# RMSNorm and matmul on one core: tile 112 stored apart from tiles 113 to 115, in two pieces of 114 and 14 rows

## The chip, the cores and the metric

One core of one Trainium2 chip runs the kernel. The metric is device time in microseconds (us) of one execution, lower is better. Beside the timed runs there is one profiled execution, whose trace has every instruction of the five engines and every packet of the 16 DMA engines that serve the core.

## The reference

The input x has 16 x 1024 rows (tokens) of 512 float32 features. Each row is divided by its root mean square, multiplied by gamma, and taken through a 512 x 768 matrix:

```
rms = np.sqrt(np.mean(x ** 2, axis=-1, keepdims=True) + eps)
x_norm = x / rms * gamma
return np.matmul(x_norm, weight).astype(np.float32)
```

The output is 16,384 rows of 768 float32 numbers, 50.3 MB; x is 33.6 MB.

## The kernel before

The 16,384 rows are cut into 128 tiles of 128 rows (one row for each of the 128 partitions). A tile's product is 128 x 768, and each partition's piece of it is 3,072 bytes.

**Work on a tile.** x is loaded in groups of 4, 8 or 16 tiles (`load`). GpSimd casts x to bf16 (`cast`, L189), ScalarE takes the sum of squares (`square`, L197) and the root of the mean (`root`, L202), and VectorE its reciprocal. TensorE transposes the tile, two features at a time as one 32-bit word (`transpose_word`, L231), and VectorE copies the result out of PSUM (`evac`, L240). For four tiles in sixteen VectorE does the transpose itself in blocks of 32 x 32 (`move`, L272). Then TensorE multiplies by the weights (`product`, L301), which have gamma folded in, into one of three accumulators. `finish_tile` scales the product by the row's reciprocal root and writes it to a slot of the output buffer `ot`: even tiles on ScalarE (L280), odd tiles on VectorE (L282).

**Stores.** `ot` has four slots of eight tiles each (`OG` = 8, `OTS` = 4), used in turn. `finish_tile` calls `store` after each tile; `store` does nothing until the last tile of a stretch is there, and then issues one DMA on the SP queue (L294). The stretches come from `stretches` at L139: usually eight tiles, in the first group 1, 1, 2 and 4, in the group of tiles 112 to 119 4 and 4, in the last group 4, 2 and 2. The tile that ends a stretch also waits for the tile before it (`before` in `finish_tile`), so that the store has one engine to wait for.

**Rows in memory.** `rows` gives a block of tiles (32 of them from tile 32 on) interleaved rows: partition p of the block's tile t is row 32 p + t of the block. A store of n tiles is therefore 128 pieces of n x 3,072 bytes, each from one partition.

**Order.** The program is listed in the order of the code, and `Order.emit` sends it to the engines: it works out for each operation which earlier ones it needs, and puts waits on semaphores ahead of it on its own engine. The engines run their lists in order and meet only at those waits. A transfer gets a semaphore of its own while it is in flight. The loop over pairs of tiles (L406) sets what is queued behind what: casts, moves, norms and loads ahead, the transposes of a later pair fed between the matmuls of the pair at hand, then the two evictions with their stores. The SP queue carries the first loads (x up to tile 31, and the weights) and all 22 stores; the ScalarE queue carries gamma and the later loads. `emit` holds back the last store (tiles 126 and 127), which is issued after the other engines' ends are arranged; the waits for stores that nothing else waits for stand on ScalarE (`left`, L440).

Of the kernel before, what the change touches and what calls it, by code (L numbers as in the profile page):

```python
# [16 lines left out]
P = 128  # L17
# [83 lines left out]
def kernel(  # L101
# [9 lines left out]
    PE, DVE, ACT, POOL, SP = nc.tensor, nc.vector, nc.scalar, nc.gpsimd, nc.sync  # L111
    order = Order(tc)
# [5 lines left out]
    out = out.flatten_outer_dims()  # L118
# [5 lines left out]
    XG, OG = 16, 8  # L124
# [3 lines left out]
    def stretches(group, parts):  # L128
        first, size, i = {}, {}, 0
        for g in range(NT // group):  # L130
            for n in parts.get(g, [group]):
                for t in range(i, i + n):
                    first[t], size[t] = i, n
                i += n
        return first, size

    last = NT // OG - 1
    x_first, x_size = stretches(OG, {0: [4, 4]})
    o_first, o_size = stretches(OG, {0: [1, 1, 2, 4], last - 1: [4, 4], last: [4, 2, 2]})  # L139

    def rows(ap, i, n):
        base, t = (i - i % OG, OG) if OG <= i < XG else (x_first[i], x_size[i]) if i < OG else (i - i % XG, XG) if i < 2 * XG else (i - i % (2 * XG), 2 * XG)
        return ap[base * P:(base + t) * P, :].rearrange("(p t) d -> p t d", t=t)[:, i - base:i - base + n, :]

    def sb(name, shape, dtype):
        return nc.alloc_sbuf_tensor(name, shape, dtype).ap()
# [11 lines left out]
    ot = [sb(f"ot{n}", [P, OG, O], F32) for n in range(OTS)]  # L158
# [10 lines left out]
    def cells(name, slot, i, n=1):  # L169
        return [(name, slot, t) for t in range(i, i + n)]  # L170
# [115 lines left out]
    def accumulator():  # L286
        return next(turns) % 3

    def store(i):
        first, n = o_first[i], o_size[i]  # L290
        s = first // OG % OTS
        if i == first + n - 1:
            src = ot[s][:, first % OG:first % OG + n, :]
            order.transfer(SP, lambda: SP.dma_start(out=rows(out, first, n), in_=src), reads=cells("ot", s, first % OG, n))  # L294

    def hold(lhsT, of):
        run(PE, lambda: PE.ldweights(lhsT), of)  # L297
# [20 lines left out]
    def finish_tile(i, a, engine):  # L318
        s = i // OG % OTS

        before = [("ot", s, i % OG - 1)] if i == o_first[i] + o_size[i] - 1 else []
        scale(engine, ot[s][:, i % OG, :], ops[a][:, :O], rstd[:, i:i + 1],
              [("ops", a, 0), ("ops", a, 1), ("rstd", i)] + before, [("ot", s, i % OG)] + (opening if i == OG * (OTS - 1) else []))
        store(i)
# [158 lines left out]
```

## Time and profile before

| What | us |
|---|---|
| median of 3 runs | 209.56 |
| lowest and highest | 209.47, 212.21 |
| profiled execution, its own time | 209.04 |
| its span, first to last instruction | 206.97 |
| TensorE busy | 194.4 (94% of the span) |
| VectorE, ScalarE, GpSimd busy | 149.4, 144.5, 59.9 |
| mean granted TensorE clock | 0.980 of full speed |
| DMA: moved 85.62 MB, mean 414 GB/s | |

The stores' DMA issues, as the trace has them (start on SP), and when all of a store's semaphore counts had come in:

| Store of tiles | issued | landed |
|---|---|---|
| 104 to 111 | 176.86 | 191.49 |
| 112 to 115 | 183.06 | 195.11 |
| 116 to 119 | 189.24 | 198.74 |
| 120 to 123 | 193.93 | 202.38 |
| 124 and 125 | 196.53 | 204.22 |
| 126 and 127 | 199.40 | 206.06 |

How to read the profile: a row of 40 digits is the span in equal slices of 5.2 us, each digit the busy share in tenths. Only work counts as busy, not waits or the issuing of DMAs. The DMA share is the mean over the core's 16 DMA engines, so one engine that works while fifteen rest is 0.06. A DMA is cut into packets, each of which goes through one engine; a packet has a start, a duration and a size in the trace, but no engine's number. The page's line on DMA queues counts the packets of SP's queue (q1: 4176 packets, 60.29 MB), of ScalarE's (q10: 1732 packets, 25.17 MB), and of instruction fetches (q8: 7 packets, q14: 5). In the list of waits a line gives the waiting engine and line, what it waited for, the sum, the number of waits and the longest.

### The profile page before, as it was taken

How to read it: one execution, taken by the hardware profiler on the slowest of the kernel's cores; microseconds unless marked ns; L12 is line 12 of the kernel's file. 1: busy time of each engine (PE TensorE's matmuls, PEld its weight loads, DVE VectorE, ACT ScalarE, POOL GpSimd, SP SyncE). 2: the span in 40 equal slices, each digit the busy share in tenths (PEclk: the TensorE clock that was granted, in tenths of full speed). 3: DMA queues.
4: the chain of work that ended last, by engine and by line, in shares of the span. 5: the costliest groups of instructions: out<-in, count | busy, mean ns of one | idle time of the engine just before them, and what ended most of it. 6: DMA issues, size and time to landing. Idle time of an engine off the chain costs nothing.

```text
span 207.0 us, 2792 instructions
## 1 busy us (share of the span) xinstructions
PE 194.4 (94%) x1236; PEld 72.6 (35%) x717; DVE 149.4 (72%) x255; ACT 144.5 (70%) x343; POOL 59.9 (29%) x34
## 2 busy tenths in 40 slices
PE   6699999999999999999999999999999999999920
PEld 0134443442343334343344334433334333433300
DVE  0446556999579975999569975999569974999510
ACT  2698898777787687777777688677877687663310
POOL 1437751157005170062405151060701507000000
PEclk9799999999999999999999999999999999999995
DMA  5999999999999999999999999999999999999992
GB/s 206 423 439 437 399 404 422 427 441 427 424 437 424 440 420 423 431 431 439 413 440 423 424 445 412 443 418 420 443 418 434 431 437 426 423 442 404 416 423 121
DMA packets 5920, 85.62 MB, mean 414 GB/s; under 512 B 658, under 2 KB 660, under 8 KB 1556
## 3 DMA queue, kind: packets, MB, share of 16 engines
q1 hardware_dynamic: 4176, 60.29, 68.9%
q10 hardware_dynamic: 1732, 25.17, 28.5%
q8 instruction: 7, 0.11, 0.2%
q14 instruction: 5, 0.04, 0.0%
HBM read 35.13 MB, written 50.33 MB: 413 GB/s over the span
## 4 chain that ended last, share of the span: by engine, by line
PE 91%; DMA 2%; DVE 1%; ACT 1%; issue 0%; SPq 0%
PE ps L301 81%; PE ps L231 10%; DMA xt<-in_x_dram 2%; DVE ot L282 0%; ACT jk L197 0%; DVE xT L240 0%; DVE w_bf L282 0%; ACT ssq L202 0%; DVE rstd L204 0%; SPq L478 0%; SPq L437 0%
## 5 line engine op out<-in xcount | busy, mean ns | idle before, releaser
L301 PE MATMUL ps<-w_bf,xT 128*128 128x512 bf16 (+1 forms) x800 | 148.3, 327 | 0.5 <-DVE w_bf L282 0.5
L280 ACT ACTIVATE ot<-ps,rstd 128x768 f32<-128x768 f32 x64 | 57.6, 900 | 46.8 <-PE ps L301 46.7
L197 ACT ACTIVATE jk<-xt 128x512 bf16<-128x512 f32 x128 | 78.7, 618 | 3.1 <-DMA xt<-in_x_dram 3.1
L189 POOL CAST xb<-xt 128x2048 bf16<-128x2048 f32 (+3 forms) x21 | 46.4, 2218 | 114.5 <-PE ps L231 56.0
L282 DVE TENSOR_SCALAR ot<-ps,rstd 128x768 f32<-128x768 f32 x64 | 64.8, 1012 | 9.7 <-PE ps L301 9.2
L297 PEld LDWEIGHTS <-xT 128*128 128x128 bf16 x400 | 39.4, 98 | 59.9 <-issue 58.3
L231 PE MATMUL ps<-ident_f,xb 128*128 128x128 f32 x200 | 54.0, 273 | 1.7 <-POOL xb L189 1.6
L240 DVE COPY xT<-ps 128x1024 bf16<-128x1024 bf16 (+1 forms) x53 | 34.5, 653 | 26.2 <-PE ps L231 25.3
L272 DVE STREAM_TRANSPOSE xTq<-xq 32x256 f32<-32x256 f32 x112 | 48.8, 435 | 1.9
L231 PEld LDWEIGHTS ps<-ident_f,xb 128*128 128x128 f32 x200 | 28.1, 141 | 46.5 <-issue 43.6
L301 PE MATMUL ps<-w_bf,xTq 128*128 128x512 bf16 x224 | 42.8, 326 | 0.0
L197 ACT ACTIVATION_READ_ACCUMULATOR jk<-xt 128x1 f32 x128 | 24.3, 190 | 0.0
L297 PEld LDWEIGHTS <-xTq 128*128 128x128 bf16 x112 | 11.0, 98 | 14.5 <-issue 14.5
L261 POOL CAST xq<-xt 128x2048 bf16<-128x2048 f32 x7 | 13.3, 1893 | 0.0
L204 DVE RECIPROCAL rstd<-ssq 128x8 f32<-128x8 f32 (+3 forms) x20 | 3.8, 192 | 7.1 <-ACT ssq L202 6.9
L202 ACT ACTIVATE ssq<-ssq,eps_sb 128x8 f32<-128x8 f32 (+3 forms) x20 | 6.0, 300 | 0.6
L301 PE MATMUL ps<-ot 128*128 128x512 bf16 x10 | 4.3, 567 | 1.4 <-DVE eps_sb L355 1.4
L280 ACT ACTIVATE w_bf<-ot,g_sb 128x768 bf16<-128x768 f32 x2 | 1.9, 935 | 1.1 <-DMA ot<-in_weight_dram 1.1
L378 DVE COPY g_sb<-ps 128x4 f32<-128x4 f32 x1 | 0.2, 160 | 3.2 <-PE ps L372 3.2
L342 ACT ACT_TABLE_LOAD x1 | 1.3, 1283 | 1.5 <-SPq L437 1.5
L282 DVE TENSOR_SCALAR w_bf<-ot,g_sb 128x512 bf16<-128x512 f32 (+2 forms) x3 | 1.4, 481 | 0.6 <-DMA ot<-in_weight_dram 0.6
L372 PEld LDWEIGHTS ps<-ident_f,ot 2*128 2x128 f32 x2 | 0.3, 200 | 2.6 <-issue 2.6
(10 smaller groups left out, 1.9 us busy)
## 6 DMA issues: line engine op xcount, KB each, us to landing
out_dram<-ot SPq DMA_DIRECT2D x13, 3072.0 KB, 22.7
xt<-in_x_dram ACTq DMA_DIRECT2D x12, 2048.0 KB, 20.1
xt<-in_x_dram SPq DMA_DIRECT2D x3, 2048.0 KB, 17.7
out_dram<-ot SPq DMA_DIRECT2D x4, 1536.0 KB, 10.8
out_dram<-ot SPq DMA_DIRECT2D x3, 768.0 KB, 7.7
xt<-in_x_dram SPq DMA_DIRECT2D x2, 1024.0 KB, 6.9
ot<-in_weight_dram SPq DMA_DIRECT2D x2, 768.0 KB, 7.0
out_dram<-ot SPq DMA_DIRECT2D x2, 384.0 KB, 20.4
```

Source lines behind the costliest of these rows:

```text
L189: run(POOL, lambda: POOL.tensor_copy(out=xb[s][:, i % 8:i % 8 + n, :], in_=src), of, cells("xb", s, i % 8, n))
L197: run(ACT, lambda: ACT.activation(out=jk[n], in_=src[:, 0, :], func=AF.Square, accum_out=ssq[:, i:i + 1]), of, [("jk", n), ("ssq", i)])
L202: run(ACT, lambda: ACT.activation(out=ssq[:, s], in_=ssq[:, s], func=AF.Sqrt, scale=1.0 / D, bias=eps_sb), [("ssq", t) for t in range(i, i ...
L204: run(DVE, lambda: DVE.reciprocal(out=rstd[:, s], in_=ssq[:, s]), [("rms", i)], [("rstd", t) for t in range(i, i + n)])
L231: run(PE, lambda: PE.transpose(out=tp[b][:, t, h, :], in_=words[:, lo:lo + P], identity=ident_f), cells("xb", s, j % 4 * 2 + t) + ["ident" ...
L240: run(DVE, lambda: DVE.tensor_copy(out=dst[:, t:t + n, :], in_=src[:, t:t + n, :]), [("tp", b)], cells("xT", j % XTS, t, n))
L261: run(POOL, lambda: POOL.tensor_copy(out=xq[s], in_=src), of, [("xq", s)])
L272: run(DVE, lambda: DVE.transpose(out=dst, in_=src), [("xq", s)], [("xTq", s, n)])
L280: run(ACT, lambda: ACT.mul(out=dst, in_=src, mul=r), reads, writes)
L282: run(DVE, lambda: DVE.tensor_single_scalar(out=dst, in_=src, scalar=r, op=mybir.AluOpType.mult), reads, writes)
L297: run(PE, lambda: PE.ldweights(lhsT), of)
L301: run(PE, lambda: PE.add_instruction(mybir.InstMatmult(name=nc.get_next_instruction_name(), engine=mybir.EngineType.PE, ins=[PE.lower_ap(r ...
```

## The change

The group of tiles 112 to 119 is stored in stretches of 1, 3 and 4 tiles where it was 4 and 4. A stretch that begins at a tile named in `DIVIDED`, which is tile 112 alone, goes out as two DMAs, one of partitions 0 to 113 and one of partitions 114 to 127. All other stores are as before.

```
-    o_first, o_size = stretches(OG, {0: [1, 1, 2, 4], last - 1: [4, 4], last: [4, 2, 2]})
+    o_first, o_size = stretches(OG, {0: [1, 1, 2, 4], last - 1: [1, 3, 4], last: [4, 2, 2]})
...
+    DIVIDED = (112,)
+    PARTS = [slice(114), slice(114, P)]
+
     def store(i):
         first, n = o_first[i], o_size[i]
         s = first // OG % OTS
         if i == first + n - 1:
-            src = ot[s][:, first % OG:first % OG + n, :]
-            order.transfer(SP, lambda: SP.dma_start(out=rows(out, first, n), in_=src), reads=cells("ot", s, first % OG, n))
+            src, dst = ot[s][:, first % OG:first % OG + n, :], rows(out, first, n)
+            for part in PARTS if first in DIVIDED else [slice(0, P)]:
+                store_rows(dst[part], src[part], cells("ot", s, first % OG, n))
+
+    def store_rows(dst, src, of):
+        order.transfer(SP, lambda: SP.dma_start(out=dst, in_=src), reads=of)
```

## The prediction

> **What bounds the kernel now.** I read the page first, for the busy shares and for how the span is filled. These are its span and its rows of 40 slices.
>
> ```profile
> span 207.0 us, 2792 instructions
> ...
> PE   6699999999999999999999999999999999999920
> ...
> DMA  5999999999999999999999999999999999999992
> GB/s 206 423 439 437 399 404 422 427 441 427 424 437 424 440 420 423 431 431 439 413 440 423 424 445 412 443 418 420 443 418 434 431 437 426 423 442 404 416 423 121
> ```
>
> Two things are full from 10 us on: TensorE, and the 16 DMA engines together. TensorE stops two slices before the end and the DMA engines go on, so the end belongs to the stores. The waits of the SP queue say so too:
>
> ```profile
> SPq L294 <- DVE ot L282: 169.8, 19, 12.0
> ...
> SPq L478 <- DMA out_dram<-ot: 6.3, 1, 6.3
> ```
>
> SP mostly waits to be given a tile to store, and at the end it waits 6.3 us for the last store (tiles 126 and 127). The timeline of SP has that store's issue at 199.40, 0.3 us after VectorE finished tile 127. The busy table by stretch shows what those 6.3 us are (columns: length, PE, PEld, DVE, ACT, POOL, granted clock, DMA share, GB/s):
>
> ```profile
> 190.00:195.00 5.00, 5.00 (x33) 1.54 (x16) 3.05 (x5) 1.71 (x2) 0.00 (x0) 1.00 0.98 415
> 195.00:199.00 4.00, 3.05 (x20) 0.78 (x8) 1.93 (x2) 0.99 (x2) 0.00 (x0) 1.00 1.00 424
> 199.00:201.00 2.00, 0.00 (x0) 0.00 (x0) 0.10 (x1) 0.00 (x0) 0.00 (x0) 1.00 0.98 409
> 201.00:202.00 1.00, 0.00 (x0) 0.00 (x0) 0.00 (x0) 0.00 (x0) 0.00 (x0) 1.00 0.97 406
> 202.00:203.00 1.00, 0.00 (x0) 0.00 (x0) 0.00 (x0) 0.00 (x0) 0.00 (x0) 0.55 0.78 326
> 203.00:204.00 1.00, 0.00 (x0) 0.00 (x0) 0.00 (x0) 0.00 (x0) 0.00 (x0) 0.50 0.31 129
> 204.00:205.00 1.00, 0.00 (x0) 0.00 (x0) 0.00 (x0) 0.00 (x0) 0.00 (x0) 0.50 0.18 74
> 205.00:206.00 1.00, 0.00 (x0) 0.00 (x0) 0.00 (x0) 0.00 (x0) 0.00 (x0) 0.50 0.07 31
> ```
>
> The share falls in steps: all sixteen engines until 202, then 0.18 from 204 to 205, which is 0.18 x 16 = 3 engines. The packets that start from 203.7 on say the same:
>
> ```profile
> DMA packets 20, 0.10 MB, mean 52 GB/s; under 512 B 3, under 2 KB 3, under 8 KB 20
> ```
>
> A store ends on each engine with one packet of 4 bytes, for the semaphore. Three of them are left here, so three engines still have work. Thirteen are through by 203.65, the three end at 205.10, 205.48 and 205.72, and the program ends 1.25 us after the last. **The end is set by three late engines**, with idle time on thirteen others. The mean of the sixteen ends is 203.4, so no shift of rows can gain more than about 2.3 us.
>
> **The change, part by part.** Every load and store here of 128 rows is cut into 16 equal shares of 8 rows: 8 data packets and one semaphore packet on each engine. Gamma's load of two rows made two packets, on two engines at once. If 114 rows too are cut into equal shares over at most 16 engines, the most that divides 114 is 6, so six engines get 19 rows each; 14 rows go to 14 engines, one row each. Of tile 112, six engines then carry 20 rows, eight carry 1, and two none, where each had 8.
>
> Prices of a packet come from the trace: 121 ns for 3,072 bytes, 234 for 6,144, 460 for 12,288, and 9 for a semaphore. On one engine a packet starts 3 or 4 ns before the one ahead ends, so each takes 117.5, 230.5, 456.5 and 5.5 ns of the engine. No packet of 9,216 bytes is in the trace; 1.5 x 230.5 = 346 from the one side and 0.75 x 456.5 = 342 from the other bound it, and I take the middle, 344. One engine's work for tiles 112 to 115 is:
> - before: 8 x 456.5 + 5.5 = 3.66 us;
> - one of the six: 19 x 0.1175 + 0.1175 + 8 x 0.344 + 3 x 0.0055 = 5.12 us, so +1.46;
> - one with a single row: 0.1175 + 2.752 + 0.011 = 2.88 us, so -0.78;
> - one without: 2.76 us, so -0.90.
>
> Issues on SP go from one to three, 0.33 us each. On SP's timeline tile 112's two lie between the store of tiles 104 to 111 (issued at 176.86) and that of 113 to 115:
>
> ```profile
> 176.86 0.33 SPq L294 DMA_DIRECT2D out_dram<-ot  x1
> ...
> 183.06 0.33 SPq L294 DMA_DIRECT2D out_dram<-ot  x1
> ```
>
> and ScalarE's eviction of tile 112 stands in its own timeline:
>
> ```profile
> 177.06 0.90 ACT L280 ACTIVATE ot<-ps,rstd 128x768 f32<-128x768 f32 x1 [0.92 <-PE ps L301]
> ```
>
> ScalarE finishes tile 112 at 177.96; SP then waits for that, issues twice by 178.7, and is free 4.4 us before tile 115 is ready. Behind it on SP stand only the later stores, whose tiles come later still. The engines hold queued work then (the store of 104 to 111 lands up to 191.5), so the earlier issue brings nothing forward and delays nothing. Without that cover the two issues would cost 0.66 us. Tile 112's wait is now on ScalarE and no longer on tile 115; its slot of ot is never written again. Two more semaphores are awaited on ScalarE after its last work, beneath the 6.3 us. I cost all of this at nothing.
>
> So the sum depends on **which engines are the late ones**. The records carry no engine number, but packets strung end to start by those 3 to 4 ns form sixteen chains. In the first load eight chains (gamma's two among them) began by 2.04 us, or behind gamma's packet of 1.16 us; the other eight began at 2.70 to 2.89 us. The three late chains are all of the second eight, as far as the chains can be followed through 20 to 50 us, where some cross. I take the first eight for the lower-numbered half and the six as part of it, as gamma's two were. One late chain is slow in nearly every packet from 36 us on (mostly 927 to 954 ns for 24,576 bytes, where others take 912). The other two each lost about 1.4 us to one 16 KB instruction fetch; the seven fetches fall on seven chains.
>
> Then the late three go to 205.72 - 0.78 = 204.94 at most, and the six to 203.65 + 1.46 = 205.11 at most. The last packet moves from 205.72 to 205.11: **0.61 us less**. If the chain ending at 203.65 is not one of the six it is up to 0.78. The profiled execution took 209.04 (span 206.97) and would take 208.43; the median of the runs shown is 209.56, 0.52 above it, so I forecast 208.95, rounded to 208.9.
>
> On the choice of engines, the Trainium skill (DMA: Bandwidth & Descriptors, "Why a DMA increments its semaphore by 16 and not by 1") says that a DMA issued from SP uses the largest number of engines up to 16 that divides its outermost size, and the lowest-numbered ones. That gives engines 0 to 5 and 0 to 13; the trace bears out 128 rows on 16 and 2 on 2, and can't show the numbers. The same page ("Latency and other measured facts") calls engines 7 and 15 the usual slow ones; by that, the slow ones are outside the six and the sum is as above.
>
> **The rivals.**
>
> 1. *A late engine is among the six*: the other sign. Chain identity before 50 us, or the half, is wrong, or in another execution a fetch falls on a loaded engine. Then the last packet is at 205.10 + 1.46 = 206.56, 206.94 or 207.18, so +0.84 to +1.46: 210.4 to 211.0. It decides as soon as one of the six ends later than 205.72 - 1.46 = 204.26 before. For it: the packets name no engine. Against: all three late chains start in the second eight.
>
> 2. *The rows are cut nearly evenly all the same* (7 or 8 of the 114 on each engine, one more of the 14): the change does not do what it says to the balance. An engine's work moves by some -0.1 to +0.2 us: 209.5 to 209.8. For it: only cuts with whole shares are in the trace. Against: the same.
>
> 3. *The 114 rows go to fewer than six engines.* On three, 38 x 0.1175 + 0.1175 + 2.77 - 3.66 = +3.69, so 203.65 + 3.69 = 207.34, +1.6: 211.2. On one, 114 x 0.1175 + 2.88 - 3.66 = +12.6 and at least 202.28 + 12.6 = 214.9, +9.2 or more: 218.7 and above. Nothing speaks for it but the odd size.
>
> 4. *Two more small transfers cost a fixed time each, in series.* From the last store's issue at 199.40 to its first completion at 202.63 are 3.23 us, of which 8 x 0.2305 = 1.84 are packets: 1.39 fixed. Twice that is +2.8: 212.3. Against: on an engine the next store's first packet follows the semaphore packet at once. The same page of the Trainium skill ("Rules for kernel authors") asks for 128 partitions and at least 1 MiB in a DMA and says that one below 64 KB is mostly overhead; the 14 rows are 43 KB, and with work queued this trace shows no such cost.
>
> **How the numbers follow.** Forecast 0.64, rival 1 0.21, rival 2 0.08, rival 3 0.04, rival 4 0.03. The forecast's own range is 208.5 to 209.3: a gain of 0.3 to 1.0, as fetches and late engines shift by a few tenths. The range is 208.4 to 210.9: it holds the forecast, rival 2 and most of rival 1, and leaves out about 0.14. About 2% is what a measurement of this kernel can tell from no change, and 2% is 205.4 below and 213.8 above. No case gains that, since 2.3 us is the most that balance could give; slower by it is rival 3 on one or two engines and the top of rival 4: faster 0.01, same 0.95, slower 0.04.
>
> **What would show it.** In the profile after, data packets should rise by 128 (six times 19 and 14, and 8 x 16 of 9,216 bytes, for 128 of 12,288), and semaphore packets by 20. If the cut is as I say, the DMA share from 204 to 205 stands above 0.18 (more engines share the tail) and ends near 205.1, and SP's last wait falls from 6.3 to about 5.7 us. If the wait grows to 7.2 or 7.8, a late engine was among the six (rival 1). If it stays at 6.3 and the steps are alike, the cut was even. TensorE's end at 198 and every wait of SP before 176 should not move; if they move, the cause is not the tail, and the prediction is wrong in its ground.

## The result and the profile after

The change made the kernel slower by 0.8%. Over 20 runs of each, the median went from 208.99 us (208.52 to 215.00) to 210.53 us (209.93 to 212.96); the ratio is 1.008, with a 95% interval of 1.0058 to 1.0102, which is 1.2 to 2.1 us. The ratios here and below are taken over the executions in the fast state alone, so they can differ a little from the ratio of the medians. The forecast was 208.9 us, a gain. The profiled execution took 210.50 us with a span of 208.4, against 209.04 and 207.0. (The median before was 209.56 in the three runs that the prediction had.)

The page of the kernel after, by the rows shown of before:

```profile
span 208.4 us, 2771 instructions
...
PE   7799999999999999999999999999999999999900
...
DMA  5999999999999999999999999999999999999981
GB/s 205 428 437 437 390 420 423 419 439 426 442 417 423 431 431 437 426 437 428 420 437 423 436 428 429 436 426 425 425 425 432 436 450 418 425 423 393 429 367 58
```

To a tenth, everything up to the last two slices is as it was. In the list of waits of SP the last wait has grown from 6.3 to 8.0 us:

```profile
SPq L301 <- DVE ot L282: 167.1, 19, 12.0
SPq L301 <- ACT ot L280: 9.2, 2, 8.4
SPq L485 <- DMA out_dram<-ot: 8.0, 1, 8.0
```

The last store was issued at 199.16 (199.40 before), so neither TensorE nor the evictions made the end later. The busy table by stretch shows the tail:

```profile
199.00:201.00 2.00, 0.00 (x0) 0.00 (x0) 0.00 (x0) 0.00 (x0) 0.00 (x0) 1.00 1.02 427
201.00:202.00 1.00, 0.00 (x0) 0.00 (x0) 0.00 (x0) 0.00 (x0) 0.00 (x0) 0.77 1.00 418
202.00:203.00 1.00, 0.00 (x0) 0.00 (x0) 0.00 (x0) 0.00 (x0) 0.00 (x0) 0.50 0.61 252
203.00:204.00 1.00, 0.00 (x0) 0.00 (x0) 0.00 (x0) 0.00 (x0) 0.00 (x0) 0.50 0.27 111
204.00:205.00 1.00, 0.00 (x0) 0.00 (x0) 0.00 (x0) 0.00 (x0) 0.00 (x0) 0.50 0.22 92
205.00:206.00 1.00, 0.00 (x0) 0.00 (x0) 0.00 (x0) 0.00 (x0) 0.00 (x0) 0.50 0.18 74
206.00:207.00 1.00, 0.00 (x0) 0.00 (x0) 0.00 (x0) 0.00 (x0) 0.00 (x0) 0.50 0.09 37
```

Before, the share fell to 0.18 (three engines) at 204 and to nothing at 205.7. Now it falls lower and earlier, 0.61 from 202 to 203 where it was 0.78, and three engines are still at work from 205 to 206. The tail is thinner and longer: the on-time engines were relieved, the late ones loaded.

The line on SP's queue fits the cut that was forecast, with 148 packets more than the 4176 before (128 of data and 20 of semaphores):

```profile
q1 hardware_dynamic: 4324, 60.30, 68.4%
```

To see which engines these are, I strung the packets of the trace into sixteen chains as in the prediction, but now the chains carry a mark: after the store of tiles 104 to 111 six have 20 packets of 3,072 bytes, eight have 1, two have none. The ends of the chains, from the trace:

```
rows of tile 112   chains   ends of their last packet, us
20                 6        203.45  203.70  204.33  205.99  206.58  207.04
1 or none          10       202.06  202.13  202.19  202.34  202.38  202.58  202.60  202.72  202.72  202.78
```

The ten in the second line run too close together to say for certain which two carry none. All three late chains are among the six. The last, at 207.04, is the chain that takes about 945 ns for 24,576 bytes where the others take 912, the steadily slow one of the prediction. Between its semaphore packet for tiles 104 to 111 and that for tiles 113 to 115 it worked from 190.68 to 195.90, 5.22 us; before the change the same chain needed 190.54 to 194.29, 3.75 us, for tiles 112 to 115. That is +1.47 us, and the prediction had priced it at +1.46. From there to its end it took 11.1 us in one kernel and 11.2 in the other.

### The profile page after: what moved, and what is told of

Same layout as the page of the kernel before. It is cut to its first block, busy times and chain, and to the rows that moved or that the text cites. A ratio compares the mean times of both kernels' runs of the same rounds, so it can differ in the third digit from the quotient of the medians.

```text
span 208.4 us, 2771 instructions
## 1 busy us (share of the span) xinstructions
PE 193.8 (93%) x1212; PEld 72.8 (35%) x717; DVE 149.3 (72%) x255; ACT 144.4 (69%) x343; POOL 59.9 (29%) x34
## 4 chain that ended last, share of the span: by engine, by line
PE 90%; DMA 2%; DVE 1%; issue 1%; ACT 1%; SPq 0%
PE ps L308 80%; PE ps L231 10%; DMA xt<-in_x_dram 2%; DVE ot L282 0%; ACT jk L197 0%; DVE xT L240 0%; DVE w_bf L282 0%; ACT ssq L202 0%; DVE rstd L204 0%; SPq L485 0%; SPq L444 0%
## 5 line engine op out<-in xcount | busy, mean ns | idle before, releaser
L308 PE MATMUL ps<-w_bf,xT 128*128 128x256 bf16 (+1 forms) x783 | 145.2, 326 | 1.1 <-DVE w_bf L282 0.2
L308 PE MATMUL ps<-w_bf,xTq 128*128 128x256 bf16 (+1 forms) x217 | 41.8, 324 | 0.4
L308 PE MATMUL ps<-ot 128*128 128x512 bf16 x10 | 4.8, 628 | 1.4 <-DVE eps_sb L362 1.4
```

The source lines that it names most:

```text
L308: run(PE, lambda: PE.add_instruction(mybir.InstMatmult(name=nc.get_next_instruction_name(), engine=mybir.EngineType.PE, ins=[PE.lower_ap(r ...
```

## The experiments

The theory after the result: **the steadily slow engine is one of the six that took 19 rows, and the end is set there.** The rivals: each further small store costs a fixed time; the late engines are an accident of one execution; the slow engine is among the six by another place in the order than the cuts say. Edits are against the kernel after, if nothing else is said.

**Tile 112 by itself, not divided.**

```
-    PARTS = [slice(114), slice(114, P)]
+    PARTS = [slice(0, P)]
```

> Tile 112 is stored by itself in one DMA of 128 rows, tiles 113 to 115 as one store: the change without the cut into 114 and 14 rows. Theory (the late DMA engines are among the six that took 19 of the 114 rows): each engine has its 8 rows again, 8 x 117.5 ns + 8 x 344 ns + 0.011 = 3.70 us against 3.66 before, so no change, 0 to +0.1 us. Rival (each further small store costs a fixed time): one of the change's two further stores is left, so about half of its loss of 1.5 us, +0.7 us.

Measured: 209.19 us against 209.28 for the kernel before on the same chip, ratio 0.9999 (0.9963 to 1.0035). No loss shows, so it is the division that costs; the interval alone just reaches the +0.7 us of the rival, and the next runs decide. In the trace the steadily slow chain carried 8 rows and ended at 205.46, as before the change (205.48); three chains of the usual speed ended behind it, the last at 207.34; this profiled execution took 210.55, over a microsecond above the median.

**Twice the bytes in the divided stores.**

```
-    o_first, o_size = stretches(OG, {..., last - 1: [1, 3, 4], ...})
+    o_first, o_size = stretches(OG, {..., last - 1: [2, 2, 4], ...})
```

> Tiles 112 and 113 are one stretch, divided into 114 and 14 rows, and tiles 114 and 115 the next: as many stores as in the change, with twice the bytes moved between engines. Theory: one of the six has 20 x 230.5 ns + 8 x 230.5 ns + 0.017 = 6.47 us where it had 3.66, so the late ones end 2.8 us later than before the change: +2.6 to +2.9 us. Rival (fixed time for each further store): the same as the change, +1.5 us.

Measured: 212.40 against 209.28, ratio 1.0145 (1.0089 to 1.0202), so +1.9 to +4.2 us. As many stores as in the change, about twice its loss: the cost goes with the bytes put on the six engines, not with the number of stores. With four executions the interval still overlaps that of the change, but the trace agrees: the six chains with the most rows are the last six, and the steadily slow one of them ends last, at 208.35 where the change had 207.04.

**120 and 8 rows.**

```
-    PARTS = [slice(114), slice(114, P)]
+    PARTS = [slice(120), slice(120, P)]
```

> Tile 112 is cut into 120 and 8 rows: equal shares are 8 rows on each of 15 engines and 1 row on each of 8, so one engine has none of tile 112, eight have 9 rows and seven have 8. Theory (late engines among the lowest-numbered, and the engine left out is not one of them): a late engine gets at most one row more, 9 x 117.5 + 8 x 344 ns + 0.017 = 3.83 against 3.66 us, so +0.1 to +0.2 us. The picture of the prediction (a late engine is the highest-numbered): that engine gains 0.9 us and the second latest sets the end, -0.2 us or so. Rival (fixed time for each further store): +1.5 us, as in the change.

Measured: 209.29 against 209.28, ratio 1.0001 (0.9970 to 1.0032). As many stores as in the change, one of them only 24 KB, and no loss; this rules out the fixed time. The +0.1 to +0.2 us of the theory and the -0.2 of the prediction's picture both lie within the interval, so the time does not tell these apart. The chains do: the steadily slow one carried 9 rows, so it is one of the first eight engines in the order of filling. It ended at 205.76 or 205.78; another chain with 9 rows ended at the other of these times. The third behind 205 us carried 8 (205.31): the other late engines are not all among the first eight.

**Sixteen small stores as labels.**

```
-    PARTS = [slice(114), slice(114, P)]
+    PARTS = [slice(n * (n - 1) // 2, n * (n + 1) // 2) for n in range(1, 16)] + [slice(120, P)]
```

> Tile 112 is cut into 16 stores, of 1, 2, 3 and so on to 15 rows and of 8 rows. With equal shares on as many engines as there are rows, lowest number first, engine 0 gets 16 rows, engine 1 15, down to engine 7 with 9, then engine 8 with 7, down to engine 15 with none: the count of 3,072-byte packets of a chain after 177 us names its engine. Theory: the three late chains carry 11 to 16 such packets (engines 0 to 5), among them the chain whose 24,576-byte packets take about 945 ns; their work grows by 11 x 117.5 + 11 x 5.5 + 2752 ns - 3.66 us = +0.45 to +1.07 us, so the time by +0.5 to +1.1 us. The picture of the prediction: the late chains carry 7 or fewer, and the time falls or stays. Rival (fixed time for each further store, 0.7 us by the change): 15 further stores, +10 us.

Measured: 209.84 against 209.28, ratio 1.0018 (0.9991 to 1.0045): at most +0.9 us for sixteen stores more than in the kernel before (38 where it has 22), not +10. The theory's +0.5 to +1.1 us overlaps the interval. The tail of this run is unlike the others:

```profile
203.00:204.00 1.00, 0.00 (x0) 0.00 (x0) 0.00 (x0) 0.00 (x0) 0.00 (x0) 0.50 0.97 399
204.00:205.00 1.00, 0.00 (x0) 0.00 (x0) 0.00 (x0) 0.00 (x0) 0.00 (x0) 0.50 0.29 117
205.00:206.00 1.00, 0.00 (x0) 0.00 (x0) 0.00 (x0) 0.00 (x0) 0.00 (x0) 0.50 0.06 25
```

From 205 on the share is 0.06, one engine of sixteen, and the packets that start after 204.5 (first line of the answer on DMA for that window) hold one semaphore packet, so one engine's end:

```profile
DMA packets 8, 0.04 MB, mean 17 GB/s; under 512 B 1, under 2 KB 1, under 8 KB 8
```

The reason is on SP: the small stores took 0.3 to 1.3 us each to issue (below), so tiles 113 to 115 were issued at 189.36, not at 183. Fifteen engines had run dry by then and began the packets of tiles 113 to 115 together, at 190.2 to 190.4. Whatever lateness they had gathered was gone, and they ended within 204.24 to 204.39. One was not dry: the chain with 950 ns for 24,576 bytes. It ended at 206.26, and between its semaphore packet for tiles 104 to 111 (190.70) and the first packet of 9,216 bytes (192.19) it carried exactly twelve packets of 3,072 bytes. By the labels that is the fifth engine in the order of filling: the stores of 5 to 15 rows, eleven of them, and that of 8.

**Four engines loaded, then five.** Two kernels:

```
-    PARTS = [slice(114), slice(114, P)]
+    PARTS = [slice(68), slice(68, P)]
```

> Tile 112 is cut into 68 and 60 rows: equal shares are 17 rows on each of four engines and 4 rows on each of fifteen. Four engines carry 21 rows, +1.58 us, eleven carry 4, -0.43 us, one none. Theory (the steadily slow engine is the fifth that a store fills, as the run with 16 small stores shows: 12 small packets): the chain with packets of about 945 ns carries 4 rows, is relieved by 0.43 us and is not last; another of the late ones, among the first four, sets the end, +0.4 to +1.1 us. Rival (the slow engine is one of the first four): that chain carries 21 rows and is last, +1.5 us.

```
-    PARTS = [slice(114), slice(114, P)]
+    PARTS = [slice(85), slice(85, 127), slice(127, P)]
```

> Tile 112 is cut into 85, 42 and 1 rows: 17 rows on each of five engines, 3 on each of fourteen, 1 on one. Five engines carry 20 or 21 rows, +1.46 to +1.58 us, nine carry 3, two none. Theory (the slow engine is the fifth): the chain with packets of about 945 ns carries 20 rows and ends last, as in the change, +1.4 to +1.6 us, and more than the run with four loaded engines. Rival (it is among the first four): the same time here as there, within 0.1 us. If it is the sixth or later, the chain carries 3 rows.

Measured on one chip, against 209.02: with four engines 209.60, ratio 1.0026 (0.9995 to 1.0056); with five 211.00, ratio 1.0087 (1.0063 to 1.0110). The fifth engine makes the difference, and five loaded engines cost what the change costs with six. In the traces the steadily slow chain carries 4 rows with four engines loaded and ends at 205.07; with five it carries 20 and ends at 206.86. So it is behind the first four and among the first five. This agrees with the twelve labels.

Two things in these traces went otherwise. In each a chain with few rows was the last, at 208.54 (4 rows) and 207.86 (3 rows). Both were over 2 us behind the bulk before tile 112, and some of their packets were longer than usual: the 4 rows took the one 1.08 us, where 0.48 is usual. From 180 us on most of their packets of 24,576 bytes had the usual 912 ns, so they are not the slow engine; why they were late in these executions is open. With four engines the profiled execution took 211.80, far above that kernel's median, so that trace shows the place of the slow engine, not the usual end.

**Labels at the start.** This kernel is the one before, with the first load of weights cut into 114 and 14 rows (what follows from the cut for the waits is left out here):

```
-        order.transfer(SP, lambda: SP.dma_start(out=w_f32[:, 2 * h:2 * h + 2, :]..., in_=wv[:, h, :]), ...)
+        for part in [slice(114), slice(114, P)] if h == 0 else [slice(0, P)]:
+            weight_rows(h, part)
```

> The kernel before, but the first load of weights, which follows the first load of x on SP's queue, is cut into 114 and 14 rows, so that six chains of packets carry 20 of its 6,144-byte packets, eight carry 1 and two none, 3 us into the run. The prediction took the chains that begin the first load early (by 2.05 us, or behind gamma's packet) for the lower-numbered half that holds the six. If that step was right, all six are early starters, and the fault was in following chains from 20 to 50 us. If it was wrong, some of the six begin at 2.6 us or later. No change of time of over 0.5 us is expected by either.

Measured: 218.90 in one run, against 209.02, so the half microsecond was a miss by far. From 5 to 15 us the loads ran at about half their rate, with all engines busy. First the kernel before, then this one:

```profile
5.00:10.00 5.00, 2.80 (x11) 0.87 (x8) 1.86 (x6) 2.95 (x7) 2.15 (x3) 0.75 1.02 428
10.00:15.00 5.00, 5.00 (x31) 1.82 (x18) 2.58 (x7) 4.74 (x13) 2.02 (x2) 0.91 1.03 439
```

```profile
5.00:10.00 5.00, 2.53 (x8) 0.82 (x6) 0.82 (x3) 1.63 (x5) 2.15 (x3) 1.00 1.00 236
10.00:15.00 5.00, 0.00 (x0) 0.00 (x0) 0.00 (x0) 0.00 (x0) 0.00 (x0) 1.00 1.03 243
```

TensorE had nothing to do from 10 to 15 us. Of the six marked chains four began the first load by 2.04 us and two at 2.68 and 2.70, but in so disturbed a stretch I do not rest on that; the next run puts the question with little disturbance.

**Light labels at both ends.** Tile 112 and the first load of weights are cut alike, the load by the edit of the run above with three parts:

```
-    PARTS = [slice(114), slice(114, P)]
+    PARTS = [slice(112), slice(112, 122), slice(122, P)]
```

> Tile 112, and the first half of the weights' load 3 us into the run, are each cut into 112, 10 and 6 rows: 7 rows on each of sixteen engines, 1 on each of ten, 1 on each of six. The six engines of the change then carry 9 rows at both ends of the run, four carry 8, six carry 7, with little imbalance. The step of the prediction on trial: the eight chains that begin the first load early hold all of the six, and a chain can be followed to the end. If it holds, the chains with 9 packets at the start are all early, and those that carry 9 at the end are the same ones. If the chains with 9 at the start are early and late starters alike, the halves were wrong; if a followed chain has 9 at one end and 7 at the other, the following was. The steadily slow chain has 9 rows at the end by the theory that it is the fifth. Time: 9 x 117.5 + 2752 + 22 ns against 3.66 us is +0.2 us by the theory; a fixed time of 0.7 us for each further store would give +2 us or more.

Measured: three of the six marked chains began the first load early (1.98 to 1.99 us) and three late (2.60 to 2.68). And when each chain was followed from its mark at the start to its mark at the end, the marks agreed on 8 chains of 16 and differed on 8; with marks of 9, 8 and 7 rows on six, four and six chains, 5.5 would agree by chance. Both halves of the step fail: the early starters are not the half that holds the six, and the following loses chains on the way. The steadily slow chain carried 9 rows at the end, as the theory has it (its end, 207.09, is the last but one). The time was 210.61 in one run, and the kernel before took 215.38 and 208.56 in one run each on that chip, so it says nothing of the tail; the load stage was again slower (292 GB/s from 5 to 10 us, not 428), which the expected +0.2 us did not have.

**The kernel before, a second trace.**

> The kernel before once more, unchanged, for a second trace of it. Theory (the fifth engine is slow in every execution): one chain again takes about 945 ns for 24,576 bytes where the others take 912, and ends among the last three, about 2 us behind the bulk; the other late chains need not end where they did. Rival (the late engines are an accident of one execution): no such chain, and other ends of the tail.

Measured: 208.56 in one run. One chain again needs more for 24,576 bytes than the 912 ns of the others (935 to 954 ns behind 177 us), and it ends last, at 205.18; two others end at 205.00 and 205.12, the remaining thirteen by 204.28. In the first trace the three ends were 205.10, 205.48 and 205.72, and the slow chain's was the second. The slow engine is there each time; the two beside it may be others each time: behind 177 us their packets of 24,576 bytes took the usual 912 ns in both traces.

## Why the prediction was wrong

1. *What bounds the kernel.* Right. The end is set by late DMA engines, and the last store was issued no later than before (199.16 against 199.40). One reading beside it was off: the line with 20 packets, given for the packets from 203.7 on, is of those from 204 on, and from 203.7 there are 25; three engines are at work in either.
2. *How the rows are cut.* Right: 19 rows on each of six engines, 14 engines with 1 row. The Trainium skill (DMA: Bandwidth & Descriptors, "Why a DMA increments its semaphore by 16 and not by 1") gives that rule, and the lowest-numbered engines for it. The counts of packets in the divided stores here agree with the rule; that the engines are the lowest-numbered no trace can show, only that the stores fill them in one order.
3. *The prices.* Right: +1.46 us priced and +1.47 measured on the slow chain; single-row and empty engines ended by 202.78, relieved as forecast. That further stores cost nothing that can be measured also held (ratios 0.9999 and 1.0001). One price was too low: the second issue on SP took 1.07 us, not 0.33; it was over at 179.27, long before the next store at 182.81, and so cost nothing. The 1.39 us that rival 4 took for a fixed time holds about 1.0 us of waiting, as no engine was through with the store before until 200.40.
4. *Which engines are late.* **This step failed**: "I take the first eight for the lower-numbered half and the six as part of it", after "The three late chains are all of the second eight, as far as the chains can be followed". By the light labels three of the six begin in the second eight, and the followed chains kept their mark in 8 cases of 16. What the runs show in its place: the steadily slow engine is the fifth that a store fills, hence one of the six; the change gave it 12 rows more, its work grew by 1.47 us, and it ended at 207.04, last of all, where it had ended at 205.48.
5. *The support from the page.* The Trainium skill (DMA: Bandwidth & Descriptors, "Latency and other measured facts") says that engines 7 and 15 are usually slower than the others and ties that, as a best guess, to DMAs issued from GpSimd. This kernel has none of these, so the rule gave the step no support, and the steadily slow engine that was measured is another: the fifth that a store fills, number 4 if the lowest-numbered are filled first.
6. *The rival that came true* is the first, at 0.21: a late engine among the six, +0.84 to +1.46 us. The measured +1.2 to +2.1 us is at its upper end and above. The slow engine alone accounts for that: it ended at 205.48 and 205.18 in the two traces before and at 207.04 after, 1.6 to 1.9 us later. In the trace after, the two other late chains were loaded ones too. The test it named was met as well, with the last wait of SP at 8.0 us where 7.2 or 7.8 was written.

The evidence for the step was one thin sign (when a chain's first packet starts) carried over 200 us by matches of 3 or 4 ns. The weight given to it, 0.64 against 0.21, was more than that bears.

Not settled: why the fifth engine is slow. As far as its chain can be followed, its packets are the longer ones from 36 us on in both queues (611 ns for 16,384 bytes elsewhere, mostly 618 to 632 here), but not in the load stage before 24 us. No version that beats both kernels was found: to relieve the fifth engine, cuts of the kind used here must load the four ahead of it, and with 68 and 60 rows that gave 1.0026 (0.9995 to 1.0056).

## What to carry to other kernels

Where the last stores set the end, look at how the DMA share falls: steps of a sixteenth tell how many engines are late, and a change of the cut is worth what it takes off the latest of them. Before loading some engines to relieve others, find out which ones are late by a mark that the trace can show, such as a store cut into 1, 2, 3 rows and so on, not by the order in which packets happen to start. A number of rows that does not split evenly over sixteen engines is a shift of load: here each row of 3,072 bytes more on the latest engine was 0.12 us.

## What the runs showed of the hardware that was not expected

- **A cut of one early load halved the rate of the loads behind it**: 236 to 243 GB/s with the DMA share at 1.00, where it was 428 to 439. The packets themselves took longer: 8,192 bytes had a median of 572 ns from 5 to 10 us, where the kernel before had 309. With the light cut it was 292 GB/s from 5 to 10 us and 430 after. Each is one run. The same cut among the stores did no such thing: from 187 to 193 us, when its packets went through, the rate was 399 GB/s where the kernel before had 418. Why is open.
- **A store issued right behind another can take three times as long to issue on SP.** A store of 128 rows by itself mostly takes 0.33 us; one of two rows and one of ten took, in the run with sixteen stores:

```profile
177.90 0.81 SPq L301 DMA_DIRECT2D out_dram<-ot  x1
```

```profile
185.55 1.29 SPq L301 DMA_DIRECT2D out_dram<-ot  x1
```

  The 14-row store of the change took 1.07 us. But it is not the few rows: the first of the sixteen, of one row, took 0.31, and of the pair of 68 and 60 rows the first took 0.32 and the second the rest of this:

```profile
178.53 1.45 SPq L301 DMA_DIRECT2D out_dram<-ot  x2
```

  Nor is it always so: from 186.9 us on, stores of 11 to 15 rows and of 8, issued one behind the other, took 0.30 to 0.44. Why is open.
- **Letting the engines run dry evens them out.** In the run with sixteen stores, fifteen chains that had run dry ended within 0.15 us of each other; in the kernel before, thirteen ended over 1.4 us and two of the usual speed later still. Its ten executions lay within 209.62 to 210.22. Those of the kernel before on that chip went from 208.70 to 211.56, and three further ones to 213.42. That the narrower spread comes from the lateness dropped before the last stores is likely, and not shown.
